# A hybrid decoder layer on one core: TensorE's instructions in the order in which the program writes them

## The chip, the core and the metric

The kernel runs on one core of a Trainium2 chip. What counts is the device time of one execution in microseconds (us); the time before is the median of three runs. The engines have short names in the rows: PE is TensorE (matmul), PEld its weight loads, DVE is VectorE, ACT is ScalarE, POOL is GpSimd, SP is SyncE, whose queue issues most loads.

## What is computed

One layer of a hybrid decoder (width 1024) over a prompt of 2048 positions and over 8 single samples that share the weights:

```python
h = rmsnorm(x, norm1_g)
z = h @ w_in                               # 2432 columns, split among four mixers
ya = chunk_gmlp(zau, zav, ...)             # 128-position chunks, causal W_s per head
yb = s5_ssm(zbu, ...)                      # 16 groups x 64 complex states
yc = short_conv(zcx, zcb, zcc, ...)
yd = rwkv7(zd, ...)                        # 4 heads x 64, delta rule
x = x + concat(ya, yb, yc, yd) @ w_out
x = x + (silu(gate) * up) @ w_down         # gate, up = rmsnorm(x) @ w_gu
y = rmsnorm(x)
```

Inside rwkv7 the key `kk` is normalised by head, a state matrix is carried from position to position, and a bonus is added to its normalised output:

```python
kk = kk / jnp.maximum(jnp.linalg.norm(kk, axis=-1, keepdims=True), 1e-12)
bonus = jnp.sum(rf * kf * r_k, axis=-1, keepdims=True) * vf
out = (on + bonus) * g
```

## The kernel before

**Large products.** The prompt is cut into four pieces of 512 positions. Every weight matrix is used in split precision: a 128x128 weight tile is cast (`wh`, ACT, L176) and its remainder is taken (`wl`, DVE, L177), and one k-tile costs three matmuls of 512 columns, one of the high parts (L214) and two of bf16 parts (L218), all written by `mmg`. The 8 samples ride in the columns of one piece (the last in the output projection and the FFN, there in two blocks of 260; piece 1 in the z projection). These products I call large. Weights stream in through SP's queue into three raw buffers. PSUM is cut into 4 buffers for large products (`m`), 3 for the mixers (`x`) and 1 for small sums (`ms`).

**The stages.** A prelude norms the input, projects the z columns of all pieces (those of pieces 1 and 2 are parked in DRAM), sets up the S5 matrices (`s5_setup`) and runs the mixers of piece 0. Then stage q runs the output projection, the second norm and the FFN of piece q (22 tiles `up`/`down`), and beside it the mixers of piece q+1. The last stage has no mixers. In the windows below the stretches are the prelude (0 to 557 us, up to the first lora product of the next piece), stages 0, 1 and 2 (to 1041, 1614 and 2218 us) and the last stage.

**A mixer.** RWKV works on half pieces z0 and z1 of 256 positions. `rw_a` makes the decay, the gates and the normalised key: lora products (L920), squares of the key (ACT), their sum by head (L960), square root, reciprocal, then the bonus product (L977) and scans. `rw_b` transposes, builds the matrix `BD` (L1069, L1070), multiplies it (L1074, L1075) and inverts a 32x32 triangle on POOL (L1103, L1105). `rw_c` is the recurrence, 8 chunks one after the other, each a chain of TensorE and DVE steps: L1128 (state times `RB`), DVE L1131, L1132 (times the inverse `Y`), copies L1133/L1134, then L1137 and L1146. `rw_d` norms the output and turns it back (L1173). `zrest` holds the gMLP (L796 among its products) and the convolution, `s5` the four groups of the state space.

**What sets the order.** A tile scheduler orders the instructions of all five engines: it simulates them with its own costs and picks by priority (`tc.high_priority(offset=...)`). The table `todo` only says at which FFN tile a mixer's part is written into the program; where its matmuls end up among the large ones the scheduler decides. Each engine then runs its own list in order, and waits on semaphores for the other engines.

Of the kernel before, what the change touches and what calls it, by code (L numbers as in the profile page):

```python
# [17 lines left out]
P = 128  # L18
# [47 lines left out]
def trunk(ctx: ExitStack, tc: tile.TileContext, I, O):  # L66
# [21 lines left out]

    def nm(s):
        uid[0] += 1  # L90
        return f"{s}_{uid[0]}"
# [46 lines left out]
    with tc.high_priority(offset=60000):  # L138
        pv = const.tile([P, NPV], F32, name="c_pv")
        nc.scalar.dma_start(pv, I["pv"])  # L140
# [12 lines left out]
    with tc.high_priority(offset=60000):  # L153
# [14 lines left out]
    def weights(srcs, hp=None):  # L168
        parts = [[] for _ in srcs]
        for i, (src, pl) in [(i, x) for i in range(2) for x in zip(srcs, parts)]:  # L170
            with tc.high_priority(offset=hp[i] if hp else HP):
# [32 lines left out]
    def mmg(jobs, mixed=False):  # L204
# [6 lines left out]
        for run in runs:  # L211
            for i, ps, blk, (wh, _, _), (xh, _, _) in run:
                for p_, (c0, n) in zip(ps, blk):
                    T.matmul(p_[:, :n], lhsT=wh, rhs=xh[:, c0 : c0 + n], start=i == 0, stop=False)  # L214
            for i, ps, blk, (_, wb, wl), (_, xb, xl) in run:
                for a, b, e in ((wl, xb, False), (wb, xl, True)):
                    for p_, (c0, n) in zip(ps, blk):
                        T.matmul(p_[:, :n], lhsT=a, rhs=b[:, c0 : c0 + n], start=False, stop=e and i == ends[id(ps)])  # L218

# [33 lines left out]
    def rms(rs, w, E_=G, pst=mst):  # L253
# [3 lines left out]
        nb = len(starts)  # L257
        ps = pst()
# [9 lines left out]
        newton(r, mc, EPS, st16()[:, :nb], E_)  # L268
        for c0 in [P * b for b in range(nw)] + ([P * nw] if nw < nb else []):
            n = min(P, w - c0)  # L270
            if c0 == TP:
                S.copy(rs[:, :TP], ps)
            o = ps[:, c0 % TP : c0 % TP + n]
            b = c0 // P
            T.matmul(o, lhsT=rt[:, b : b + 1].to_broadcast([P, P]), rhs=ident[:, P - n :], start=True, stop=True)
        c0 = TP if w > TP else 0
        S.copy(rs[:, c0:w], ps[:, : w - c0])
        return rs, rt, ps
# [18 lines left out]
    def norm0():  # L297
# [3 lines left out]
        for i in range(2):  # L301
            with tc.high_priority(offset=(30000, 5000)[i]):
# [7 lines left out]
        with tc.high_priority(offset=-2000):  # L310
            return h, rms(squares(lambda k: xs[k], TP, at_, True), TP)
# [17 lines left out]
    with tc.high_priority(offset=20000):  # L329
        h, (rs0, rt0, _) = norm0()  # L330
# [12 lines left out]

    wsum = mst()
    for i in range(4):
        T.matmul(wsum[64 * (i % 2) : 64 * (i % 2) + 64, P * (i // 2) : P * (i // 2) + P],
                 lhsT=ones.to_broadcast([P, 64]), rhs=wst[:, i], start=True, stop=True)
    for j in range(2):
        t = tri[:, P * j : P * j + P]
        V.tensor_scalar(t, wsum[:, P * j : P * j + P], 1024.0, col("gl", j), op0=ALU.mult, op1=ALU.mult)  # L350
        V.tensor_tensor(bsb[:, j], bsb[:, j], t, op=ALU.add)
# [48 lines left out]


# [7 lines left out]
    def s5_setup():  # L409
        with ExitStack() as c2:  # L410
# [120 lines left out]
            def cmul(ore, oim, ar, ai, br_, bi_):  # L531

                tt(tmp, b16(ar), br_, ALU.mult)
                tt(tmp2, b16(ai), bi_, ALU.mult)
                tt(ore, tmp, tmp2, ALU.subtract)
                tt(tmp, b16(ar), bi_, ALU.mult)
                tt(tmp2, b16(ai), br_, ALU.mult)
                tt(oim, tmp, tmp2, ALU.add)
# [44 lines left out]
            for i in range(2):  # L583
# [8 lines left out]
                Fz.append(f_)  # L592
            for pr in range(8):
# [4 lines left out]
                for g in range(2):  # L598
                    ps_ = slice(64 * g, 64 * g + 64)
                    for ri in range(2):  # L600
# [4 lines left out]
                        else:  # L605
                            act(cv[ps_, ri, g], bc[ps_, 3, pr], AF.Copy, scale=-1.0)
                            act(fv[ps_, ri, :, g], Ft[ps_, 1, pr], AF.Copy, scale=-1.0)
                pe = mst()
# [39 lines left out]

    def park(h, q):
# [22 lines left out]
    def zload(h, m, q, off=0):  # L672
# [4 lines left out]
        for p_, (c0, n) in zip(ztile(h, m, q), zblocks(q)):  # L677
            if q == 0 and m < 2:
                S.copy(t[:, off + c0 : off + c0 + n], p_[:, :n])
                V.tensor_tensor(t[:, off + c0 : off + c0 + n], t[:, off + c0 : off + c0 + n], rs0[:, c0 : c0 + n], op=ALU.mult)  # L680
            elif q == 0:
# [5 lines left out]
    def zrw(h, q):  # L687
        w = zwidth(q)
        zs = rw.tile([P, 7, TP], F32, tag="zs", name=nm("zs"))

# [23 lines left out]
    def zrest(h, q, cct):  # L714
# [14 lines left out]

# [5 lines left out]
        pst = mst if q in parked else mmt  # L735
        uu = [] if q in parked else [gate(j) for j in range(2)]
        if q not in parked:
            wv = [weight(I["wv"][i]) for i in range(2)]
        vn = []
        for g, (b0, nb, rows) in enumerate(groups(q)):  # L740
            vt = zt_() if rows == P else vs
            n = 256 * nb
            if q in parked:
                nc.sync.dma_start(vt[:rows, :n], zdr[q - 1, 17 + g, :rows, :n])
                act(vt[:rows, :n], vt[:rows, :n], AF.Gelu_apprx_tanh)
            else:
                ps = zav(h, b0 * P, nb, rows, wv)
                for b in range(nb):
                    act(vt[:, b * 256 : b * 256 + 256], ps[:, b * 256 : b * 256 + 256],
                        AF.Gelu_apprx_tanh, scale=rt0[:, b0 + b : b0 + b + 1])  # L750
            for b in range(nb):
                vb = vt[:rows, b * 256 : b * 256 + 256]
                bn = st16()
                V.bn_stats(bn[:rows, 0:6], vb)
                V.bn_aggr(bn[:rows, 6:8], bn[:rows, 0:6])
# [867 lines left out]
```

## Time and profile before

| | before |
|---|---|
| median of 3 runs | 2649.69 us (2646.79 to 2650.6) |
| the profiled execution | 2644.79 us, its span 2643.0 us |
| PE busy | 2451.2 us, 93% of the span |
| DVE busy | 1781.7 us, 67% |
| ACT busy | 1063.5 us, 40% |
| POOL busy | 935.9 us, 35% |
| mean granted clock of TensorE | 0.955 of full |

The span runs from the first to the last instruction. An engine that is busy for 93% of it is the one that sets the time; what is left to win on it are its waits, the time in which it ran at the lower clock, and the work itself.

### The profile page before, as it was taken

The page shows a single profiled execution, that of the slowest core. Times are in us where ns is not written, and L with a number is a line of the kernel's source. Part 1 is how long each engine was busy: PE and PEld are TensorE (multiplying, and loading weights), DVE is VectorE, ACT ScalarE, POOL GpSimd, SP SyncE. Part 2 cuts the span into 40 slices and gives each one's busy share as a digit, 9 for nine tenths or more (in the row PEclk, how much of TensorE's full clock was granted, in tenths as well). Part 3 has the DMA queues.
Part 4 walks back from the last instruction along what each step waited for, and adds up shares of the span by engine and source line. Part 5 has one row for each costly group of instructions (what it writes and reads, how often), then busy time and mean ns, then how long its engine had stood idle before and what let it go on. Part 6 is the DMA issues. An engine that isn't in the chain of part 4 may idle for free.

```text
span 2643.0 us, 39426 instructions
## 1 busy us (share of the span) xinstructions
PE 2451.2 (93%) x13863; PEld 1632.7 (62%) x14020; DVE 1781.7 (67%) x3213; ACT 1063.5 (40%) x2173; POOL 935.9 (35%) x1358
## 2 busy tenths in 40 slices
PE   7778989999889999999899999989899999999998
PEld 4557975655455654555555545655455557888887
DVE  6694463488677667876776668556876686566666
ACT  5543443453433334444333345533443335322223
POOL 8588350035346112471371133351362114111102
PEclk9798999999879999999899998999999999999999
DMA  4224444432313223423232235332432234232332
GB/s 135 77 80 153 163 131 133 145 100 76 117 51 109 86 89 116 141 74 121 70 114 81 91 120 160 108 115 85 124 110 84 92 94 158 91 97 93 96 93 80
DMA packets 179606, 280.94 MB, mean 106 GB/s; under 512 B 39208, under 2 KB 53584, under 8 KB 179408
## 3 DMA queue, kind: packets, MB, share of 16 engines
q1 hardware_dynamic: 161648, 254.50, 31.0%
q10 hardware_dynamic: 17760, 23.91, 2.6%
q8 instruction: 110, 1.80, 0.3%
q14 instruction: 88, 0.72, 0.1%
HBM read 250.24 MB, written 28.10 MB: 105 GB/s over the span
## 4 chain that ended last, share of the span: by engine, by line
PE 60%; POOL 14%; DVE 11%; issue 5%; DMA 4%; ACT 3%; SPq 0%; ACTq 0%; POOLq 0%; DVEq 0%
PE m L218 34%; PE m L214 18%; POOL BD L1105 4%; POOL inv L1103 4%; DVE wl L177 2%; POOL s5Q L423 1%; DVE g L867 1%; PE x L1137 1%; PE x L1146 1%; DMA z<-zdr 1%; PE x L1074 1%; POOL inv L423 1%; PE x L1128 1%; DVE xm L1290 1%; DMA x<-in_xq 1%
## 5 line engine op out<-in xcount | busy, mean ns | idle before, releaser
L218 PE MATMUL m<-rl,wh 128*128 128x512 bf16 (+1 forms) x2741 | 839.7, 337 | 9.6 <-DVE rl L284 1.7
L177 DVE TENSOR_TENSOR wl<-raw,wh 128x512 bf16<-128x512 f32 x744 | 571.4, 777 | 394.3 <-ACT wh L176 390.3
L218 PE MATMUL m<-rh,wl 128*128 128x512 bf16 (+1 forms) x2660 | 832.1, 345 | 2.2 <-issue 0.9
L176 ACT CAST wh<-raw 128x512 fp32r<-128x512 f32 x744 | 450.4, 617 | 937.9 <-PE m L218 699.0
L214 PE MATMUL m<-rh,wh 128*128 128x512 f32 (+1 forms) x2760 | 643.8, 374 | 30.5 <-ACT rh L197 15.1
L218 PEld LDWEIGHTS <-wl 128*128 128x128 bf16 x3640 | 351.3, 98 | 368.5 <-issue 119.5
L214 PEld LDWEIGHTS m<-rh,wh 128*128 128x128 f32 x2760 | 452.4, 192 | 126.3 <-ACT rh L197 18.9
L218 PEld LDWEIGHTS <-wh 128*128 128x128 bf16 x3640 | 361.1, 99 | 232.0 <-issue 15.2
L1273 POOL TENSOR_TENSOR gr<-gp,rs 128x512 f32<-128x512 f32 (+1 forms) x110 | 144.5, 1321 | 722.9 <-DVE gp L1271 641.9
L214 PE MATMUL m<-ah,wh 128*128 128x512 f32 (+1 forms) x880 | 289.9, 419 | 22.7 <-DVE xm L1290 11.2
L1290 DVE TENSOR_TENSOR xm<-m,xm 128x512 f32<-128x512 f32 (+1 forms) x440 | 249.0, 581 | 91.5 <-PE m L218 89.9
L218 PE MATMUL m<-al,wh 128*128 128x512 bf16 (+1 forms) x877 | 287.3, 342 | 3.2 <-issue 0.7
L218 PE MATMUL m<-ah,wl 128*128 128x512 bf16 (+1 forms) x845 | 285.2, 352 | 0.6 <-DVE wl L177 0.5
L1127 POOL TENSOR_SCALAR stl<-st,g 128x64 f32<-128x64 f32 x128 | 73.2, 587 | 348.3 <-DVE st L1140 344.5
L214 PEld LDWEIGHTS m<-ah,wh 128*128 128x128 f32 x880 | 151.1, 193 | 67.5 <-DVE xm L1290 18.1
L1103 POOL TENSOR_TENSOR inv<-BD 32x30 f32<-32x30 f32 (+14 forms) x240 | 148.1, 617 | 74.4 <-DMA BD<-dl 56.2
L1105 POOL TENSOR_TENSOR BD<-BD,inv 32x30 f32<-32x30 f32 (+14 forms) x240 | 155.0, 646 | 18.3
L244 POOL TENSOR_TENSOR rs<-rs,at 128x512 f32<-128x512 f32 (+1 forms) x53 | 76.7, 1448 | 114.4 <-ACT at L133 110.7
L1274 DVE SCALAR_TENSOR_TENSOR ft<-ft,gr 128x512 f32<-128x512 f32 (+1 forms) x110 | 77.2, 716 | 52.3 <-POOL gr L1273 47.1
L1271 DVE TENSOR_TENSOR gp<-m,rs 128x512 f32<-128x512 f32 (+1 forms) x110 | 62.3, 582 | 23.5 <-PE m L218 21.2
L1276 ACT CAST ah<-ft 128x512 fp32r<-128x512 f32 (+1 forms) x88 | 54.7, 621 | 52.5 <-DVE ft L1275 50.1
L1275 DVE SCALAR_TENSOR_TENSOR ft<-ft,m 128x512 f32<-128x512 f32 (+1 forms) x110 | 61.9, 578 | 20.5 <-PE m L218 20.1
(371 smaller groups left out, 2800.8 us busy)
## 6 DMA issues: line engine op xcount, KB each, us to landing
raw<-in_wgu SPq DMA_DIRECT2D x352, 256.0 KB, 2.6
raw<-in_wd SPq DMA_DIRECT2D x176, 256.0 KB, 2.6
raw<-in_wz SPq DMA_DIRECT2D x136, 256.0 KB, 2.7
raw<-in_wo SPq DMA_DIRECT2D x64, 256.0 KB, 2.7
x<-in_xq SPq DMA_DIRECT2D x40, 256.0 KB, 3.1
zdr<-zp ACTq DMA_DIRECT2D x33, 256.0 KB, 2.2
z<-zdr SPq DMA_DIRECT2D x33, 256.0 KB, 3.3
xm<-in_xq SPq DMA_DIRECT2D x24, 256.0 KB, 4.0
```

The lines of the kernel that those rows point to most:

```text
L176: S.copy(hi, raw)
L177: (G if spare[0] and i > 9 else V).tensor_tensor(lo, raw, hi.bitcast(F32), op=ALU.subtract)
L214: T.matmul(p_[:, :n], lhsT=wh, rhs=xh[:, c0 : c0 + n], start=i == 0, stop=False)
L218: T.matmul(p_[:, :n], lhsT=a, rhs=b[:, c0 : c0 + n], start=False, stop=e and i == ends[id(ps)])
L244: G.tensor_tensor(acc[:, :w], acc[:, :w], sq[:, :w], op=ALU.add)
L1103: G.tensor_tensor(tv, xtv[:, 0:s, s : s + 1].to_broadcast([32, s, r]), xtv[:, s : s + 1, s + 1 :].to_broadcast([32, s, r]), op=ALU.mult)
L1105: G.tensor_tensor(xtv[:, 0:s, s + 1 :], xtv[:, 0:s, s + 1 :], tv, op=ALU.add)
L1127: G.tensor_scalar(stl[:, j], old[:, j], pvw[:, 8 * j + c, 32:33], None, op0=ALU.mult)
L1271: V.tensor_tensor(gp[:, c], pss[0][b][:, :n], rs[:, c], op=ALU.mult)
L1273: G.tensor_tensor(gr[:, c], gp[:, c], rs[:, c], op=ALU.mult)
L1274: V.scalar_tensor_tensor(tv, tv, 1.0, gr[:, c], op0=ALU.add, op1=ALU.mult)
L1290: V.tensor_tensor(xm[m][:, c0 : c0 + n], p_[:, :n], xm[m][:, c0 : c0 + n], op=ALU.add)
```

## The change

TensorE is taken out of the scheduler: within `tc.manual_schedule` its instructions run in the order in which the program writes them. The other four engines are still ordered by the scheduler.

The order is now made in the program. A mixer's part, a norm or a gate is a Python generator in a `Strand`, and it yields a number where it needs the result of another engine. `mmg` calls `tick` after each large product (a product of 512 columns counts 1, of 256 one half), and `tick` resumes every strand whose number has run out. So between two steps of a strand stand a fixed count of large products, if there are any: `Strand.done` and `finish` run what is left of a strand with none between. RWKV yields 50 between the squares of the key and L1097 (L960 before), 36 and then 24 and 10 in `rw_b`, 13 at each of the three steps of a chunk (10 in piece 0), 36 before the transposes of `rw_d`; a norm yields 24 between its sums (L326) and its broadcast (L342).

Besides that:
- The bonus product (L977) moves from `rw_a` to `rw_tail`, the end of the half piece (L1134); the two lora products of a half are issued together.
- At the start, the first four z tiles of piece 0 are written ahead of the first norm's remaining steps (`ahead0`). The first two z columns of piece 0 are no longer copied by ACT before they are scaled.
- 48 products of 128x128 elements in `s5_setup` (`cmul`) go from POOL to DVE, as does one multiply of piece 0's keys per half; some adds of the second norm's squares and its last steps go to DVE as well. In all DVE runs 82 more TENSOR_TENSOR, 8 more TENSOR_SCALAR and 8 fewer SCALAR_TENSOR_TENSOR, POOL 74 and 8 fewer; ACT loads its table 66 times instead of 57. TensorE's matmuls and the DMAs stay the same in number.
- The gate bias, the final multiplies of the pieces and the samples' mixer become strands too.

Core of the diff:

```diff
+    ctx.enter_context(tc.manual_schedule(engines={mybir.EngineType.PE}))
...
+    def tick(n=1.0):
+        now[0] += n
+        for t in list(strands):
+            if not t.over and t.wake <= now[0]:
+                t.step()
...
             for i, ps, blk, (wh, _, _), (xh, _, _) in run:
                 for p_, (c0, n) in zip(ps, blk):
                     T.matmul(p_[:, :n], lhsT=wh, rhs=xh[:, c0 : c0 + n], start=i == 0, stop=False)
+                tick(sum(n for _, n in blk) / 512)
...
-                tt(tmp, b16(ar), br_, ALU.mult)
+                V.tensor_tensor(tmp, b16(ar), br_, op=ALU.mult)
...
+        if q == 0:
+            ahead0.extend(ztile(h, m, q) for m in range(4))
+            first.done()
...
+        yield 50 if n == 256 else 20
+        yield from free()
         ps = pst()
         T.matmul(ps[:, : 2 * n], lhsT=blk1, rhs=sq, start=True, stop=True)
...
-    def bonus(zs, c0, n, kf, out, t, pst):
+    def bonus(zs, c0, n, kf, t):
...
-        ps = pst()
-        T.matmul(ps[:, : 2 * n], lhsT=blk1, rhs=t, start=True, stop=True)
...
+        ps = pst()
+        T.matmul(ps[:, : 2 * n], lhsT=blk1, rhs=bon, start=True, stop=True)
...
+        gap = 10 if q == 0 else 13
         for c in range(8):
...
+            yield gap
             T.matmul(pu[:, :64], lhsT=Y[:, c], rhs=z_, start=True, stop=True)
...
+    m.done()
     spare[0] = False
...
-            todo = {0: [nx.a1], 2: [nx.c0], 4: [nx.b1], 5: [nx.rest], 8: [lambda: nx.s5(0)], 9: [lambda: nx.s5(1)],
-                    10: [lambda: nx.s5(2)], 11: [lambda: nx.s5(3)], 13: [nx.c1]}
...
+            if nx and i == 3:
+                nx.start_rest()
...
+            nx.done()
```

In RWKV's strand (`rwkv` in class `Mix`) the parts now follow as:

```python
z0 = yield from rw_a(q, 0, self.zs)
yield from rw_b(z0)
yield 24
z1 = yield from rw_a(q, 1, self.zs)
yield 180
yield from rw_c(z0)
...
yield from rw_b(z1)
...
yield 250
yield from rw_c(z1)
```

**TensorE, the end of the recurrence.** Before, in stage 0, the last chunks of piece 1's second half stand in TensorE's list without a large product between them (`st` is the state, `Y` the inverse):

```order
L1128 MATMUL x_6326<-st_6300,RB 128x64 x2
L1132 MATMUL x_6327<-z_6325,Y 128x64
L1137 MATMUL x_6328<-uv_5302,bt_5317 128x64
L1146 MATMUL x_6326<-uv_5302,sc_5316 128x64
L1137 MATMUL x_6328<-uv_5302,bt_5317 128x64
L1146 MATMUL x_6326<-uv_5302,sc_5316 128x64
L1128 MATMUL x_6349<-st_6323,RB 128x64 x2
```

The changed kernel has the same recurrence as lines L1275, L1280, L1286 and L1295; this is one chunk of the same half in stage 0, with the FFN's products (`m`) around it:

```order
L1275 MATMUL x_6815<-st_6718,RB 128x64 x2
L269 MATMUL m_6836<-rh_5780,wh_6826 128x512 x4
L269 MATMUL m_6836<-rh_5780,wh_6832 128x512 x4
...
L274 MATMUL m_6836<-rl_5781,wh_6826 128x512
L1280 MATMUL x_6816<-z_6814,Y 128x64
L274 LDWEIGHTS wl_6827
...
L269 MATMUL m_6888<-rh_5780,wh_6878 128x512 x3
L1286 MATMUL x_6817<-uv_5457,bt_5472 128x64 x2
L1295 MATMUL x_6815<-uv_5457,sc_5471 128x64 x2
L269 MATMUL m_6888<-rh_5780,wh_6878 128x512
L269 MATMUL m_6888<-rh_5780,wh_6884 128x512 x4
```

From L1275 to L1280 stand 14 large products now, from L1280 to L1286 13, and from L1295 to the next L1275 13.

**DVE, the start of the program.** Before, the first z tile that is taken out of PSUM on DVE (L682, `m` times the norm's `rs`) stands ahead of the samples' state products that need `s5s`, a result of `s5_setup` on POOL:

```order
L697 SCALAR_TENSOR_TENSOR zs_257<-z_288,c_pv,z_258 128x512
L696 TENSOR_TENSOR z_336<-z_294 128x512
L682 TENSOR_TENSOR z_339<-m_352,rs_154 128x512
L177 TENSOR_TENSOR wl_481<-raw_478,wh_480 128x512
L697 SCALAR_TENSOR_TENSOR zs_257<-z_336,c_pv,z_294 128x512
L696 TENSOR_TENSOR z_380<-z_339 128x512
L848 TENSOR_TENSOR ns_7647<-s5s,c_s_226 128x16
L851 TENSOR_TENSOR ns_7647<-s5s,c_s_226 128x16
L848 TENSOR_TENSOR ns_7803<-s5s,c_s_226 128x16
```

In the changed kernel all twelve state products (L971 to L976) stand ahead of the first such z tile, now L778:

```order
L232 TENSOR_TENSOR wl_466<-raw_463,wh_465 128x512
L971 TENSOR_TENSOR ns_7877<-s5s,c_s_198 128x16
L974 TENSOR_TENSOR ns_7877<-s5s,c_s_198 128x16
...
L975 TENSOR_TENSOR ns_8117<-s5s,c_s_198 128x16
L976 TENSOR_TENSOR ns_7877<-ns_7877 128x16
L976 TENSOR_TENSOR ns_8117<-ns_8117 128x16
L778 TENSOR_TENSOR z_387<-m_230,rs_156 128x512
L795 TENSOR_TENSOR z_391<-z_387 128x512
L778 TENSOR_TENSOR z_397<-m_267,rs_156 128x512
```

The twelve moved from behind the first z tile to ahead of all of them. On TensorE 96 large products (four tiles of 24, one for each `m` buffer) can be written before a buffer has to come free.

**TensorE, the end of the prelude.** In the changed kernel `m.done()` writes what is left of piece 0's second half behind the last large product of the prelude:

```order
L274 MATMUL m_4987<-wl_4902,rh_3763 128x256
L1280 MATMUL x_5040<-z_5038,Y 128x64
L1286 MATMUL x_5041<-uv_3648,bt_3663 128x64 x2
L1295 MATMUL x_5039<-uv_3648,sc_3662 128x64 x2
L1275 MATMUL x_5073<-st_5036,RB 128x64 x2
...
L1275 MATMUL x_5096<-st_5070,RB 128x64 x2
L1280 MATMUL x_5097<-z_5095,Y 128x64
L1286 MATMUL x_5098<-uv_3648,bt_3663 128x64 x2
L1295 MATMUL x_5096<-uv_3648,sc_3662 128x64 x2
L1324 MATMUL x_5127<-c_ident,g_5116 128x128 x4
L1134 MATMUL x_5140<-g_1386,c_blk_101 128x512
L1043 MATMUL x_5147<-zs_229,c_lora 128x256 x2
```

What stands there without a large product between is two thirds of a chunk, two whole chunks, `rw_d`'s turn (L1324), the bonus (L1134) and the last lora product (L1043); before, those chunks stood among the z projection's products.

## Rows read from the trace of the kernel before

**Rows 1.** The page: busy us (share of span) and instructions by engine.

```profile
PE 2451.2 (93%) x13863; PEld 1632.7 (62%) x14020; DVE 1781.7 (67%) x3213; ACT 1063.5 (40%) x2173; POOL 935.9 (35%) x1358
```

**Rows 2.** Windows of the five stretches: busy us, granted clock, DMA share.

```profile
core 0: us, PE busy (x) PEld busy (x) DVE busy (x) ACT busy (x) POOL busy (x), PEclk, DMA share, GB/s
0.00:557.00 557.00, 487.72 (x2872) 344.62 (x2894) 325.94 (x615) 248.73 (x563) 285.27 (x523) 0.92 0.41 127
557.00:1041.00 484.00, 449.47 (x2164) 271.57 (x2205) 346.33 (x638) 187.43 (x389) 164.27 (x230) 0.93 0.29 89
1041.00:1614.00 573.00, 523.85 (x2465) 306.93 (x2509) 418.98 (x699) 238.88 (x469) 226.73 (x282) 0.95 0.34 108
1614.00:2218.00 604.00, 578.30 (x2854) 345.11 (x2904) 418.86 (x738) 252.22 (x495) 189.29 (x247) 0.99 0.34 106
2218.00:2643.00 425.00, 411.91 (x3519) 364.42 (x3518) 271.63 (x525) 136.22 (x259) 70.31 (x79) 0.99 0.31 96
```

**Rows 3.** Windows of four stretches with the clock at 0.50, and their sum.

```profile
...
724.70:758.80 34.10, 22.78 (x91) 17.93 (x89) 19.72 (x68) 6.76 (x23) 10.02 (x33) 0.50 0.11 32
sum 92.20, PE 64.28 PEld 49.74 DVE 59.37 ACT 32.26 POOL 32.21; mean PE 16.07 PEld 12.43 DVE 14.84 ACT 8.07 POOL 8.05
```

**Rows 4.** Waits of PE: line, releaser, us in total, times, longest.

```profile
PE x L977 <- DVE g L974: 22.7, 4, 10.1
...
PE ms L796 <- DVE z L759: 14.1, 3, 7.1
...
PE x L1173 <- DVE g L1170: 6.3, 1, 6.3
```

**Rows 5.** PE timeline: start, us, work, in brackets idle before and releaser.

```profile
725.53 0.69 PE L1132 MATMUL x<-z,Y 128*128 128x64 f32 x2 [0.54 <-DVE z L1131]
...
730.16 0.69 PE L1132 MATMUL x<-z,Y 128*128 128x64 f32 x2 [0.54 <-DVE z L1131]
```

**Rows 6.** PE timeline, one z tile of 24 products.

```profile
74.66 2.21 PE L214 MATMUL m<-rh,wh 128*128 128x512 f32 x8
76.72 0.40 PE L218 MATMUL m<-rh,wl 128*128 128x512 bf16 x1
```

**Rows 7.** Window of 21 bf16 products of 512 columns.

```profile
76.70:81.36 4.66, 4.59 (x21) 2.04 (x22) 1.61 (x2) 0.00 (x0) 4.19 (x10) 1.00 0.21 68
```

**Rows 8.** PE and ACT timeline: lora products, then the squares for L960.

```profile
1040.60 1.14 PE L920 MATMUL x<-zs,c_lora 32*128 32x256 f32 x8
...
1066.04 0.50 ACT L133 ACTIVATE g<-zs,c_pv 128x256 f32<-128x256 f32 x1
...
556.90 1.14 PE L920 MATMUL x<-zs,c_lora 32*128 32x256 f32 x8
...
570.60 0.91 ACT L133 ACTIVATE g<-zs,c_pv 128x256 f32<-128x256 f32 x2
```

**Rows 9.** PE and DVE timeline: L960, then the half's last BD write.

```profile
1079.37 1.02 PE L960 MATMUL x<-g,c_blk 128*128 128x512 f32 x2
...
1109.39 0.84 DVE L1069 TENSOR_TENSOR BD<-g,g 64x256 f32<-64x256 f32 x2
...
1630.57 1.02 PE L960 MATMUL x<-g,c_blk 128*128 128x512 f32 x2
...
1648.86 0.42 DVE L1069 TENSOR_TENSOR BD<-g,g 64x256 f32<-64x256 f32 x1
```

**Rows 10.** PE, POOL and DVE timeline of the start.

```profile
5.28 0.80 PE L214 MATMUL m<-rh,wh 128*128 128x512 f32 x1 [5.28 <-ACT rh L133]
...
17.16 0.69 POOL L418 TENSOR_SCALAR t<-s5raw 128x8 f32<-128x8 f32 x1 [3.79 <-DMA s5raw<-in_s5l]
...
45.02 0.36 POOL L423 TENSOR_TENSOR s5s<-t,t 128x8 f32<-128x8 f32 x2
...
45.26 0.18 DVE L848 TENSOR_TENSOR ns<-s5s,c_s 128x16 f32<-128x16 f32 x1 [1.76 <-POOL s5s L423]
```

**Rows 11.** Groups of POOL by line: count, busy us, mean ns, idle before.

```profile
L423 POOL TENSOR_TENSOR s5tmp<-s5s,s5G 128x128 f32<-128x128 f32 x12 | 7.2, 622 | 0.5
```

More of the change, by code (lines that the diff above doesn't have):

```diff
@@ L87, in trunk, with __init__, __enter__, __exit__ @@
     uid = [0]
+    ctx.enter_context(tc.manual_schedule(engines={mybir.EngineType.PE}))
+    offs = [0]
+    strands = []
+    now = [0.0]
+    class hp:
+        def __init__(self, o):
+            self.o = o
+        def __enter__(self):
+            self.cm = tc.high_priority(offset=self.o - offs[0])
+            self.old, offs[0] = offs[0], self.o
+            self.cm.__enter__()
+        def __exit__(self, *a):
+            self.cm.__exit__(*a)
+            offs[0] = self.old
+    class Strand:
+        def __init__(self, gen, prio, wait=0.0, norm=False):
+            self.gen, self.prio, self.wake, self.over = gen, prio, now[0] + wait, False
+            self.norm = norm
+            strands.append(self)
+        def step(self):
+            with hp(self.prio):
+                d = next(self.gen, None)
+            if d is None:
+                self.over = True
+                strands.remove(self)
+            else:
+                self.wake = now[0] + d
+    def tick(n=1.0):
[3 more added lines that the diff above has]
+                t.step()
+    def finish(*ts):
+        while any(not t.over for t in ts):
+            for t in [t for t in strands if t in ts or t.norm]:
+                if not t.over:
+                    t.step()
+    def wait_for(*cond):
+        while not all(c() for c in cond):
+            yield 4
     def nm(s):
@@ L218, in mmg @@
                         T.matmul(p_[:, :n], lhsT=a, rhs=b[:, c0 : c0 + n], start=False, stop=e and i == ends[id(ps)])
+                tick(sum(n for _, n in blk) / 256)
     def newton(r, m, eps, t, E_=G):
@@ L399, in trunk, with gate_bias @@
     parked = set()
+    def gate_bias():
+        yield from ms_free()
+        wsum = mst()
+        for i in range(4):
+            T.matmul(wsum[64 * (i % 2) : 64 * (i % 2) + 64, P * (i // 2) : P * (i // 2) + P],
+                     lhsT=ones.to_broadcast([P, 64]), rhs=wst[:, i], start=True, stop=True)
+        for j in range(2):
+            t = tri[:, P * j : P * j + P]
+            V.tensor_scalar(t, wsum[:, P * j : P * j + P], 1024.0, col("gl", j), op0=ALU.mult, op1=ALU.mult)
+            V.tensor_tensor(bsb[:, j], bsb[:, j], t, op=ALU.add)
     s5_e = dr.tile([8, P, 256], F32, name="s5_e")
@@ L963, in rw_elem @@
         V.reciprocal(sq, sq)
[L964 removed]
+        (G if n == 256 and not first else V).tensor_tensor(kkn, kkn, sq, op=ALU.mult)
         kf = sq
@@ new lines, in start, with start_rest, take, rwkv @@
+        def start(self, wait=0):
+            self.rw = Strand(self.rwkv(), RP, wait)
+        def start_rest(self, wait=0):
+            self.ot = Strand(self.others(), MP, wait)
+        def take(self):
+            if self.cct is None:
+                self.cct = ring_tile()
+            return self.cct
+        def rwkv(self):
+            q = self.q
+            yield from wait_for(lambda: all(f.over for f in finals))
+            z0 = yield from rw_a(q, 0, self.zs)
[4 more added lines that the diff above has]
+            yield from rw_c(z0)
+            yield from wait_for(lambda: self.cct is not None)
+            yield from rw_d(z0, self.cct)
+            yield from rw_b(z1)
+            self.half = True
+            yield 250
+            yield from rw_c(z1)
+            yield from wait_for(lambda: self.s5_over)
+            yield from rw_d(z1, self.cct)
@@ L1451, in trunk @@
-    for pg in range(4):
-        m.s5(pg)
-    if last > 1:
-        with tc.high_priority(offset=2 * RP):
-            h1 = norm1(2, rs1)
-        with tc.high_priority(offset=-LOW):
-            park(h1, 2)
-    m.c1()
+    with hp(MP):
+        n1 = Rms(norm1_squares(1), zwidth(1), prio=MP, wait=100)
+    with hp(MP):
+        m.gm2 = m.rest()
+        next(m.gm2)
+    with hp(2 * RP):
+        h = norm1(1, n1.done())
+    m.start_rest(30)
+    if last > 1:
+        with hp(MP):
+            n1 = Rms(norm1_squares(2), zwidth(2), prio=MP, wait=200)
```

455 lines of the change are left out of this document (254 added, 201 removed).

## The prediction

> **What bounds the kernel.** I read the busy shares first, then windows cut at the stage borders, then TensorE's waits, then single places in the timeline. TensorE is busy 2451.2 us of 2643.0, DVE 1781.7 [rows 1]: TensorE sets the time. The windows [rows 2] show where it does not work at full rate: it idles 69.3 us in the prelude (557.00 less 487.72), then 34.5, 49.2, 25.7 and 13.1 us. The granted clock adds a second loss. It stands at one of two levels, so a mean of 0.92 over 557 us means 2 x 0.08 x 557 = 89 us at half clock; for the other windows 68, 57, 12 and 9 us. In four long half-clock stretches TensorE is busy 64.28 of 92.20 us [rows 3], 70%; half of that work time would be saved at full clock, so a half-clock us costs about 0.35 us: 31, 24, 20, 4 and 3 us. (Bounds: if all idle time lies in half-clock time, the prelude loses 10 us this way; if none, 45. The others 17 to 34, 4 to 29, 0 to 6.) Idle and clock loss together are 100, 58, 69, 30 and 16 us, 273 in all; the rest, about 2370 us, is work that the change does not touch, since TensorE's matmuls stay the same in number.
>
> The waits have no single cause. The largest is the bonus product, 22.7 us in four waits, the longest 10.1; others are the gMLP product (14.1 in three) and the end of a half piece (6.3) [rows 4]. Where the recurrence runs out of large products it takes 4.63 us a chunk (730.16 less 725.53) [rows 5]; the stretch in which it does so, 724.7 to 758.8, has the clock at 0.50 and 22.78 of 34.10 us busy [rows 3].
>
> **The change, part by part.** The measure of cover is the large product. A z tile's 8 products of the high parts take 76.72 less 74.66, 0.26 us each [rows 6], 21 bf16 products 4.66 us, 0.22 each [rows 7]; over a tile of 24 that is 0.233 us, the price of one tick.
>
> *Recurrence.* Three hops of 13 ticks give a chunk 9.1 us of large products, against 4.63 us that it needs alone. In stages 0 to 2 every chunk stands so, and their waits and most half-clock time in these stretches should go.
>
> *Key norm.* 50 ticks are 11.7 us. From the lora products to the squares it takes 24.8 us in one half (1041.74 to 1066.54) and 13.5 in another (558.04 to 571.51) [rows 8]. The first is at a loose place, where nobody hurried DVE; I take a shortfall of 2 us a half, bounds 0 and 13.2.
>
> *BD.* From L960 to the last write of BD it takes 29.8 us (1080.39 to 1110.23) or 17.7 (1631.59 to 1649.28) [rows 9]; 36 and 24 ticks are 14.0 us. Shortfall 3.7 by the tighter row, 15.8 by the other, 0 if the scheduler puts this chain ahead of its other DVE work; I take 3.
>
> *Bonus.* At the end of its half nothing waits between its operands and itself, so the 22.7 us of [rows 4] go. Its result is now needed at once by the multiply in the tail, which only the output product waits for; in stages that is hidden by the FFN.
>
> *Other strands* (norms, gMLP, S5, the FFN's own evacuations). A single gMLP wait is 4.7 us today [rows 4]. I leave 8 us a stage, bounds 2 and 16.
>
> So stages 0, 1 and 2 keep 2 x 2 + 2 x 3 + 8 = 18 us of waits and 4 of half clock, 22 each. They gain 36, 47 and 8. The last stage has no mixer and gains nothing.
>
> *The prelude* gains less, for two places. At the start TensorE begins at 5.28 us and can write 96 products before it needs a buffer: 22.4 us, and some 3 more at its early rate, so it stands at about 31. The evacuation it needs is now behind the state products that want `s5s`, which POOL writes at 45.02 to 45.38 [rows 10]. That is a wait of 14 us that was not there before (the first z tile was taken ahead of those). Bounds: 8 if the S5 load, waited for 3.79 us at 17.16 [rows 10], comes earlier, 20 if POOL, which now does the norm later, is later too. At the end, 2.7 chunks of 4.63 us, `rw_d` with a wait like the 6.3 us at L1173 [rows 4], and a tail that I put at 5 us stand alone: 24 us, at a clock that falls. The first 5.3 us stay, the two halves of piece 0 fall short by 12 together (their counts are shorter), 7 for the rest, 5 of half clock: 5 + 14 + 24 + 12 + 7 + 5 = 67, a gain of 33.
>
> *Work moved to DVE.* 48 products of 128x128 leave POOL, where such ones took 0.622 us with little idle time before them [rows 11]. On DVE they add at most 48 x 0.62 = 30 us to 1781.7; TensorE waits for neither, as the S5 matrices are wanted late, so I cost them at nothing. If that cover is gone, a few of the 30 us appear in the prelude. The Trainium skill says in "SBUF — State Buffer", section "SBUF: two separate sides", that DVE and GpSimd share a port pair under an exclusive lock: a DVE instruction with two SBUF inputs and a GpSimd instruction wait for each other in full. By it each moved product could be held for one POOL instruction, another 30 us of DVE time and up to that much on the total; no row here separates such holding from work, and the sum goes without it.
>
> Sum: 33 + 36 + 47 + 8 = 124. The profiled execution took 2644.8 us, 1.8 more than its span, and lies 4.9 below the median of the three runs. 2644.8 - 124 = 2521, and 2526 on the median's scale; I say 2525.
>
> **The rivals.**
> (a) *The cover suffices nearly everywhere.* For it: the last window idles only 13.1 us of 425 with a written-like list. Then a stage keeps 5 us instead of 22 and the prelude 39 (start, tail, 10 for the rest): gains 61 + 53 + 64 + 25 = 203, 2447 on the median's scale. Against it: the counts of [rows 8] and [rows 9].
> (b) *The waits move to the queues of DVE and ACT.* These still run their own lists in the order that the scheduler thinks right, and each hop needs one result from them. In stage 1 DVE is busy 418.98 of 573 us [rows 2]. If each of the 3 x 16 x 3 = 144 hops of the stages misses its time by 0.5 us, as now at L1132 (0.54 [rows 5]), that is 72 us: 2598.
> (c) *Slower: a late small product holds all large ones behind it.* Today the scheduler placed a mixer's product late enough for its own model; now TensorE stands in front of it. Place: L1097 and the first product of BD, in each of eight halves. With the loose durations, 13.2 and 15.8 us short, a half loses 29 instead of the 4 to 6 taken above: some 190 us more, 2715. It decides from about 15 us more a half on, half of that difference. Against it: these durations were loose because nothing on TensorE waited for them. The Trainium skill ("TensorE: Matmul & The Clock Gate", section "The mechanism") says that matmuls start and end strictly in order and only weight loads are pulled ahead, which is what would make each such wait count in full; the trace agrees at the bonus product, where nothing ran for 10.1 us.
> (d) *The change does little:* the scheduler's other four lists hold the waits as they are, 2640 to 2655.
>
> **How the numbers follow.** My forecast, with 2475 to 2570 as its own range, has 0.50; (a) 0.22, (b) 0.20, (c) 0.05, (d) 0.03. The range runs from 2440, (a) with a little more, to 2600, the end of (b); it leaves out (c), (d) and the ends of (a) and (b), under 2 in 10. About 0.2% (5 us) is what a measurement of this kernel can tell from no change. Faster: 0.50 + 0.22 + 0.20 and a little of (d), 0.93; same 0.02; slower 0.05.
>
> **What would show it.** Right: no wait at the bonus product; chunks of 9 us with large products in them and a granted clock of 0.98 or more from 557 us on; idle time of stages 0 to 2 under 25 us each; a wait of some 14 us of TensorE for an `m` buffer before 46 us; 24 us of idle and half clock at the prelude's end. Wrong: waits of 10 us and more at L1097 or L1219 in most halves (c), many short ones at L1280 and L1286 (b), or a prelude as long as before.

## The result

The changed kernel takes 2711.47 us (median, 2707.71 to 2714.41), the kernel before 2648.34 in the same session: a ratio of 1.0237, interval [1.0219, 1.0255]. It is slower by some 63 us where I forecast 124 us less. The span of the profiled execution grew from 2643.0 to 2709.7 us, by 66.7.

The page of the kernel after, its engines' busy time, which answers to [rows 1]:

```profile
PE 2453.5 (91%) x14020; PEld 1630.7 (60%) x14020; DVE 1809.0 (67%) x3295; ACT 1083.9 (40%) x2188; POOL 882.4 (33%) x1276
```

TensorE is busy 2453.5 us, as before (2451.2); what grew is the time in which it is not, from 191.8 to 256.2 us. Both kernels have one landmark at the same work: the first result of the output projection of stage 0, and the last result of the down projection of stages 0, 1 and 2. Windows cut there, first of the kernel before, then of the one after (busy us by engine, granted clock, DMA share, GB/s):

```profile
0.00:522.00 522.00, 452.91 (x2719) 325.81 (x2739) 293.16 (x568) 231.12 (x525) 269.77 (x512) 0.91 0.40 127
522.00:1058.80 536.80, 499.14 (x2378) 297.38 (x2420) 396.80 (x710) 217.10 (x459) 190.82 (x250) 0.94 0.30 93
1058.80:1582.20 523.40, 485.67 (x2316) 286.57 (x2357) 379.74 (x649) 210.20 (x410) 202.86 (x261) 0.96 0.33 102
1582.20:2207.20 625.00, 590.82 (x2844) 348.76 (x2897) 432.28 (x757) 259.89 (x509) 194.21 (x254) 0.97 0.34 108
2207.20:2643.00 435.80, 422.71 (x3612) 374.13 (x3611) 279.75 (x534) 145.16 (x274) 78.20 (x85) 0.99 0.32 101
```

```profile
0.00:550.00 550.00, 455.45 (x2746) 324.34 (x2747) 323.54 (x642) 232.59 (x537) 240.90 (x467) 0.89 0.39 123
550.00:1071.90 521.90, 481.18 (x2405) 289.37 (x2404) 381.46 (x685) 217.76 (x442) 182.40 (x236) 0.97 0.31 95
1071.90:1610.00 538.10, 484.73 (x2365) 286.03 (x2363) 381.46 (x664) 226.66 (x430) 195.55 (x253) 0.95 0.32 99
1610.00:2258.10 648.10, 595.08 (x2898) 349.34 (x2899) 442.48 (x767) 262.45 (x511) 192.26 (x247) 0.96 0.33 103
2258.10:2709.70 451.60, 437.05 (x3612) 381.59 (x3610) 280.08 (x542) 144.43 (x271) 71.26 (x75) 0.99 0.30 96
```

The prelude lost 28.0 us (550.0 against 522.0), stage 0 won 14.9, stage 1 lost 14.7, stage 2 23.1 and the last stage 15.8. In the prelude and in stages 1 and 2 the difference is idle time for the most part: 94.6 instead of 69.1, 53.4 instead of 37.7, 53.0 instead of 34.2 us. In stage 0 idle time grew a little too (40.7 instead of 37.7); what it won is busy time, 18.0 us less, at a clock of 0.97 instead of 0.94. Elsewhere the clock did not rise: 0.89 in the prelude, 0.95 and 0.96 in stages 1 and 2, against 0.91, 0.96 and 0.97. In the last stage the loss is not idle time: TensorE idles 14.6 instead of 13.1 us there, and is busy 14.3 us longer for as many matmuls (3612).

What TensorE waits for now, the answer to [rows 4] (line, releaser, us in total, times, longest):

```profile
PE m L269 <- ACT rh L252: 53.1, 24, 5.7
PE x L1097 <- ACT g L188: 35.4, 6, 9.0
PE ms L902 <- DVE z L883: 29.5, 3, 13.2
PE x L1219 <- DVE BD L1213: 20.1, 3, 12.2
PE m L269 <- DVE xm L1453: 18.1, 9, 6.5
...
PE x L1219 <- issue: 6.4, 1, 6.4
...
PE x L1280 <- DVE z L1278: 5.7, 5, 2.5
```

The bonus product is gone from the list, and the recurrence (L1280) is low. In their place stand five kinds: the parts `rh` of the normed input of the next piece, 53.1 us; the key norm's product L1097, 35.4 in six of eight halves; the gMLP product L902, 29.5 in all three stages; the first product of BD, L1219, 26.5 (with the 6.4 for which the trace shows no releaser); and evacuations of the FFN. The parts `rh` were waited for before as well, but less:

```profile
PE m L214 <- ACT rh L197: 15.1, 9, 5.9
```

Of the changed kernel's 53.1 us most are in the prelude; the same row for its window 0 to 550:

```profile
PE m L269 <- ACT rh L252: 39.6, 16, 5.7
```

### The profile page after: what moved, and what is told of

Its sections match the earlier page's. It is cut to its first block, busy times and chain, and to the rows that moved or that the text cites. A ratio compares the mean times of both kernels' runs of the same rounds, so it can differ in the third digit from the quotient of the medians.

```text
span 2709.7 us, 39564 instructions
## 1 busy us (share of the span) xinstructions
PE 2453.5 (91%) x14020; PEld 1630.7 (60%) x14020; DVE 1809.0 (67%) x3295; ACT 1083.9 (40%) x2188; POOL 882.4 (33%) x1276
## 4 chain that ended last, share of the span: by engine, by line
PE 65%; POOL 11%; DVE 11%; DMA 5%; issue 4%; ACT 3%; SPq 0%; POOLq 0%; ACTq 0%; DVEq 0%
PE m L274 37%; PE m L269 20%; POOL BD L1251 4%; POOL inv L1249 4%; DVE wl L232 2%; DMA x<-in_xq 2%; PE x L1219 1%; DMA z<-zdr 1%; DVE g L986 1%; PE x L1295 1%; PE x L1286 1%; PE x L1275 1%; ACT wh L231 1%; POOL rs L301 1%; PE ms L1034 1%
## 5 line engine op out<-in xcount | busy, mean ns | idle before, releaser
L274 PE MATMUL m<-rh,wl 128*128 128x512 bf16 (+1 forms) x2760 | 875.5, 350 | 0.0
L274 PE MATMUL m<-rl,wh 128*128 128x512 bf16 (+1 forms) x2760 | 849.3, 340 | 2.6 <-DVE rl L372 2.6
L269 PE MATMUL m<-rh,wh 128*128 128x512 f32 (+1 forms) x2760 | 651.4, 376 | 68.5 <-ACT rh L252 53.1
L1453 DVE TENSOR_TENSOR xm<-m,xm 128x512 f32<-128x512 f32 (+1 forms) x440 | 246.3, 581 | 105.0 <-PE m L274 95.8
L269 PE MATMUL m<-ah,wh 128*128 128x512 f32 (+1 forms) x880 | 249.7, 399 | 35.9 <-DVE xm L1453 16.0
L274 PE MATMUL m<-al,wh 128*128 128x512 bf16 (+1 forms) x880 | 273.2, 341 | 1.6 <-DVE al L1440 1.6
L1249 POOL TENSOR_TENSOR inv<-BD 32x30 f32<-32x30 f32 (+14 forms) x240 | 154.6, 644 | 197.3 <-DMA BD<-dl 130.6
L301 POOL TENSOR_TENSOR rs<-rs,at 128x512 f32<-128x512 f32 (+1 forms) x41 | 58.3, 1422 | 71.7 <-ACT at L188 70.8
L1438 DVE SCALAR_TENSOR_TENSOR ft<-ft,m 128x512 f32<-128x512 f32 (+1 forms) x110 | 61.9, 579 | 25.2 <-PE m L274 24.4
```

The costliest lines, as they stand in the source:

```text
L301: G.tensor_tensor(acc[:, :w], acc[:, :w], sq[:, :w], op=ALU.add)
L1249: G.tensor_tensor(tv, xtv[:, 0:s, s : s + 1].to_broadcast([32, s, r]), xtv[:, s : s + 1, s + 1 :].to_broadcast([32, s, r]), op=ALU.mult)
L1453: V.tensor_tensor(xm[m][:, c0 : c0 + n], p_[:, :n], xm[m][:, c0 : c0 + n], op=ALU.add)
```

## The experiments

Times are medians, and each ratio is to the kernel before in the same session. That kernel's own median went from 2643.81 to 2648.34 us between sessions, so a difference of two medians can be off by some 4 us; where that matters I give the difference by the ratios as well.

**Give TensorE back to the scheduler.** First with nothing else changed:

```diff
-    ctx.enter_context(tc.manual_schedule(engines={mybir.EngineType.PE}))
```

> The changed kernel with TensorE given back to the scheduler; all other edits stay. If the written order of TensorE is what costs (theory A), the 64 us of extra idle time go with it: 2620 to 2655 us. If the other edits (work moved to DVE, the strands' later writing of norms and final multiplies, the longer lists of DVE and ACT) are what costs (theory B), it stays at 2690 or above.

2685.96 us, 1.0152 [1.0136, 1.0169]: between the two theories, and not a clean undo. Its windows show why: prelude 611.3 us, stage 0 501.2. The change had also raised the priority of the parked z columns, which says nothing to a written list of TensorE, but much to the scheduler: as I read it, it finished them first and left piece 0's mixers alone at the end. So once more, with that priority as before:

```diff
-    ctx.enter_context(tc.manual_schedule(engines={mybir.EngineType.PE}))
...
-    with hp(2 * RP):
+    with hp(-LOW):
         park(h, 1)
...
-        with hp(2 * RP):
+        with hp(-LOW):
             park(h, 2)
```

> As the run with TensorE given back to the scheduler, and the parked z columns of pieces 1 and 2 put back to low priority as in the kernel before. That run lost 89 us in the prelude and won 35 and 12 in stages 0 and 1. If the prelude's loss was that priority alone: 2640 to 2655, as the kernel before. If the changed program is slower whoever orders TensorE: 2675 to 2690.

2601.54 us, 0.984 [0.982, 0.9861]: faster than either kernel, and outside both expectations. Its prelude takes 504.8 us. So the other edits are worth some 42 us under the scheduler, and the written order with these counts costs 110 us against the scheduler in nearly the same program; the lower priority of the parked columns holds for the other four engines too, and no run tried it with the written order. How the scheduler avoids the waits is seen where the key norm is latest. PE and ACT timeline of that version in stage 1: lora products, the squares, the key norm's product (here L1096):

```profile
1015.71 1.31 PE L1042 MATMUL x<-zs,c_lora 32*128 32x256 f32 x8
...
1070.35 0.91 ACT L187 ACTIVATE g<-zs,c_pv 128x256 f32<-128x256 f32 x2 [0.36 <-DVE g L1077]
...
1071.31 1.13 PE L1096 MATMUL x<-g,c_blk 128*128 128x512 f32 x2 [0.97 <-ACT g L187]
```

From the lora products' end to the squares' it took 54.2 us, and TensorE waited 0.97 us: the scheduler had put the product as late as its operands. The same place in the changed kernel:

```profile
1086.02 1.14 PE L1043 MATMUL x<-zs,c_lora 32*128 32x256 f32 x8
...
1106.54 0.91 ACT L188 ACTIVATE g<-zs,c_pv 128x256 f32<-128x256 f32 x2 [0.33 <-DVE g L1078]
...
1107.50 2.07 PE L1097 MATMUL x<-g,c_blk 128*128 128x512 f32 x2 [8.98 <-ACT g L188]
```

Here the squares end 20.3 us after the lora products, much sooner, and TensorE waits 8.98: it stands after 50 large products, 11.7 us, whatever the other engines do.

**The bonus product alone**, moved in the kernel before:

```diff
-        bonus(zs, c0, n, kf, bon, tb, mxt)
+        bonus(zs, c0, n, kf, bon)
...
         ps = pst()
+        T.matmul(ps[:, : 2 * n], lhsT=blk1, rhs=bon, start=True, stop=True)
+        for j in range(2):
+            V.tensor_tensor(bon[:, j * n : j * n + n], ps[:, j * n : j * n + n], zs[:, 5 + j, c0 : c0 + n], op=ALU.mult)
+        ps = pst()
         lora_mm(ps, 64, 128, zs, c0, n)
```

> The kernel before with the bonus product alone moved to the end of its half piece. If the 22.7 us of waits at the bonus product were a loss of their own: 2622 to 2635 us. If the scheduler merely parked other late products there (the next wait takes over): 2643 to 2655.

2646.85 us, 1.0004 [0.9994, 1.0013]: nothing. Its 22.7 us of waits were a place where the list stood anyway; other waits took over, such as that of the recurrence for the inverse (4.8 us in the kernel before), here L1131:

```profile
PE x L1131 <- DMA Y<-dx: 19.0, 4, 9.8
```

In the scheduler's version of 2601.54 us I made the move back (the same edit the other way round):

> The version of 2601 us (scheduler orders TensorE, parked columns last) with the bonus product moved back to its old place. If the move helps in this program: 2610 to 2625. If it is worth nothing, as in the kernel before: 2597 to 2606.

2609.53 us, 0.9859 [0.9844, 0.9874]: between the two expectations, 8 us slower by the medians and 5 by the ratios, whose intervals overlap; so a gain from the move is not clear of noise. The bonus product (here L1113) waits again:

```profile
PE x L1113 <- DVE g L1110: 23.1, 4, 8.1
```

And the small products of the S5 set-up, put back on GpSimd in that version:

```diff
-                V.tensor_tensor(tmp, b16(ar), br_, op=ALU.mult)
+                tt(tmp, b16(ar), br_, ALU.mult)
...
-        (G if n == 256 and not first else V).tensor_tensor(kkn, kkn, sq, op=ALU.mult)
+        (G if n == 256 else V).tensor_tensor(kkn, kkn, sq, op=ALU.mult)
```

> The same version with the 48 small products of the S5 set-up and piece 0's key multiply back on GpSimd. If moving them to DVE is what shortens its prelude by 17 us: 2612 to 2625. If not: 2597 to 2606.

2614.46 us, 0.9878 [0.9863, 0.9892]: 13 us by the medians, 10 by the ratios, the first expectation. I had costed that move at nothing.

**The last stage: one output tile per group.**

```diff
-            g = 2
+            g = 2 // len(bl)
```

> The changed kernel; in the last stage the down projection takes one output tile (two PSUM buffers) per group of products instead of two (all four buffers). If the last stage is longer by 15.8 us because each group needs all four buffers back at once: 2695 us, and 859 instead of 827 matmuls per 100 us in its middle. If it is longer for another reason (weights, DVE): no change, 2711.

2698.97 us, 1.0205 [1.0188, 1.0222]. The median fell by 12.5 us (8.5 by the ratios), the last window from 451.7 to 435.7. One hundred us from the middle of the last stage, of the kernel before, the changed one and this one (matmuls in brackets):

```profile
2400.00:2500.00 100.00, 100.00 (x859) 88.48 (x858) 65.12 (x126) 29.29 (x54) 11.43 (x12) 1.00 0.30 94
```

```profile
2455.00:2555.00 100.00, 100.00 (x829) 87.13 (x827) 61.72 (x119) 28.16 (x52) 11.39 (x12) 1.00 0.29 94
```

```profile
2440.00:2540.00 100.00, 100.00 (x863) 89.30 (x861) 64.39 (x126) 29.11 (x54) 11.40 (x12) 1.00 0.30 95
```

All three are 100% busy at full clock, yet the changed kernel gets 829 matmuls done instead of 859; with one tile per group it is 863. The down projection writes groups of two output tiles by two blocks, so each group begins with eight high products into all four `m` buffers. TensorE and DVE timeline of the changed kernel, the high products of two groups and the emptying of the buffers between them (L1453):

```profile
2484.93 1.61 PE L269 MATMUL m<-ah,wh 128*128 128x260 f32 x8
...
2488.13 1.61 PE L269 MATMUL m<-ah,wh 128*128 128x260 f32 x8
...
2487.39 1.67 DVE L1453 TENSOR_TENSOR xm<-m,xm 128x260 f32<-128x260 f32 x4 [1.53 <-PE m L274]
...
2488.30 0.43 DVE L1453 TENSOR_TENSOR xm<-m,xm 128x260 f32<-128x260 f32 x1
...
2488.78 0.72 PE L269 MATMUL m<-ah,wh 128*128 128x260 f32 x2
```

The last two rows are single records out of the merged ones: the third emptying, and the fifth and sixth high product.

The kernel before, where the scheduler had put two high products at a time:

```profile
2400.08 0.49 PE L214 MATMUL m<-ah,wh 128*128 128x260 f32 x2
...
2400.79 0.49 PE L214 MATMUL m<-ah,wh 128*128 128x260 f32 x2
```

And the run with one tile per group:

```profile
2441.31 0.72 PE L269 MATMUL m<-ah,wh 128*128 128x260 f32 x4
2442.71 0.72 PE L269 MATMUL m<-ah,wh 128*128 128x260 f32 x4
```

A group of 24 products takes 3.20 us in the changed kernel (2488.13 less 2484.93); as many take 2.84 us before (four times 0.71) and 2.80 with one tile per group (twice 1.40). The last stage has 44 such groups, so by these rows an estimated 16 to 18 us, where the windows show 15.8 and 16.0. That it is the size of the group is shown by the run. That the buffers are what it waits for is seen in the single records: the fifth and sixth high product of a group, the first into its third and fourth buffer, start at 2488.78 and 2489.12, each 0.05 us behind the end of that buffer's emptying (2488.73 and 2489.06). The trace records no idle time for it.

**Longer counts, one at a time.**

```diff
-        yield 50 if n == 256 else 20
+        yield 100 if n == 256 else 20
```

> The changed kernel with 100 instead of 50 large products ahead of the key norm's product L1097. If its 35.4 us of waits come from a chain of some 21 us against 11.7 us of cover: those waits under 8 us, 2680 to 2690. If the wait only moves to the next late step (the first product of BD, the gMLP): 2703 to 2715.

2701.87 us, 1.0219 [1.0204, 1.0235]: 10 us by the medians, 5 by the ratios, neither expectation. L1097 no longer waits at all, but L902 waits 21.6 us more, in the waits of this run:

```profile
PE ms L902 <- DVE z L883: 51.1, 3, 22.8
```

```diff
-        yield 40
+        yield 120
         for j in range(2):
             yield from ms_free()
```

> The changed kernel with 120 instead of 40 large products ahead of the gMLP product L902. If its 29.5 us of waits are a count that is too short: 2685 to 2697. If they pass to the next late step of the same strand: 2703 to 2715.

2692.81 us, 1.0179 [1.0163, 1.0196]: 19 us (15 by the ratios). L902 waits no more, L1097 as before (34.9 us).

**And less cover, the dose the other way.**

```diff
-        yield 50 if n == 256 else 20
+        yield 25 if n == 256 else 20
```

> The changed kernel with 25 instead of 50 large products ahead of the key norm's product, so 5.8 us less cover in each of eight halves. If a wait in a list in written order counts in full: waits at L1097 grow by 35 to 46 us and the time with them, 2735 to 2757. If TensorE's waits merely shift between steps: 2705 to 2722.

2735.22 us, 1.0335 [1.0319, 1.035]: 24 us slower, at the edge of the first expectation. Its waits:

```profile
PE x L1097 <- ACT g L188: 80.9, 8, 17.0
...
PE ms L902 <- DVE z L883: 13.6, 3, 6.4
```

L1097 waits 45.5 us more, close to eight times the 5.8 us that were taken away. L902 waits 15.9 less and L1219 13.0 less, as I read it because their chains get on while TensorE stands at L1097; L1324 waits 17.0 more (22.9). The wait counts in full at its place, and part of it is taken off others.

**Both counts, and three mends.** If a wait at one place shortens waits elsewhere, mending it alone uncovers those, and both mends together are worth more than their sum. At the key norm and the gMLP:

```diff
-        yield 50 if n == 256 else 20
+        yield 90 if n == 256 else 20
...
-        yield 40
+        yield 120
```

> The changed kernel with the two longer counts alone (90 ahead of the key norm, 120 ahead of the gMLP product), the last stage as it was. Apart they gave 10 and 18 us. If each, mended alone, passed its waits on to the other: 2647 to 2656, as the three mends less the last stage's 12 to 16. If the three mends' 73 us need the last stage too: 2675 to 2685.

2655.65 us, 1.003 [1.0017, 1.0044]: 56 us, where apart they gave 10 and 19 (by the ratios 55, 5 and 15). L1097 waits 1.0 us in all, L902 is gone from the list. TensorE's idle time, 256.2 us in the changed kernel, is 253.1 with the key norm mended, 248.4 with the gMLP and 217.4 with both; the other 20.6 us of the span's gain are busy time, at a mean clock of 0.959 instead of 0.949. With the last stage's mend (`g = 2 // len(bl)`) as well:

> The changed kernel with three mends together: the down projection one tile at a time in the last stage, 90 products ahead of the key norm, 120 ahead of the gMLP product. Alone they gave 12, 10 and 18 us. If these are separate losses: 2668 to 2675. If a mended wait passes on to the next late step: 2680 to 2695.

2638.36 us, 0.9969 [0.9957, 0.9982]: 73 us less than the changed kernel, and a little faster than the kernel before, with TensorE in written order. It beat both expectations, the plain sum included.

**The prelude's end.**

```diff
-        gap = 10 if q == 0 else 13
+        gap = 7 if q == 0 else 13
...
-            yield 180
+            yield 60 if q == 0 else 180
...
-            yield 250
+            yield 150 if q == 0 else 250
```

> As the run with three mends, and piece 0's recurrence starts sooner (60 and 150 instead of 180 and 250 products ahead of it, 7 instead of 10 at its hops), so that its end stands among the parked z columns. If the 24 us of half clock and 12 us of idle time at the prelude's end come from those last chunks standing alone: 12 to 20 us faster than that run. If the inverse on GpSimd is not ready by then: TensorE waits at L1280 and it is no faster or slower.

2624.86 us, 0.9917 [0.9899, 0.9935]: 13.5 us less; up to the first output projection it takes 527.9 instead of 557.9 us, of which stage 0 gives 7 back. Its last chunk now stands among the parked columns, where the run with three mends has no large product for 42.6 us (497.8 to 540.4) and the changed kernel for 23.7 (510.7 to 534.4). So the longer counts had lengthened this end, and the 13.5 us are the gain over that. On top of it longer counts in `rw_b`:

```diff
-        yield 36
+        yield 60
...
-            yield (24, 10)[g % 2]
+            yield (40, 16)[g % 2]
```

> As the run with piece 0's recurrence sooner, and 60, 40 and 16 instead of 36, 24 and 10 large products in rw_b. Its waits at the first products of BD are 12.3 us in all. If that is a loss of its own: 2608 to 2618. If the waits pass on, or piece 0's end is late again: 2620 to 2640.

2644.46 us, 1.0003 [0.999, 1.0016]: 20 us slower, a little beyond the second expectation. Every product of cover also delays what follows in its strand. BD no longer waits, but in piece 0's second half the inverse on GpSimd starts at 390.2 instead of 346.9 us, and TensorE stands 15.0 us for it at once:

```profile
PE x L1280 <- DMA Y<-dx: 15.0, 1, 15.0
```

**The normed input earlier.** `norm1` for pieces 1 and 3 is made in a strand of its own, ahead of the last products that don't need it, and the first z weights are asked for behind it:

```diff
+        def done(self):
+            finish(self.n.strand, self.strand)
+            early.extend(weight(I["wz"][m]) for m in range(2))
+            return self.h
...
+            if n1 and i == 21:
+                h = norm1(q + 2, n1.done())
```

> The changed kernel with the normed input h of pieces 1 and 3 made while other large products still run (a strand during the z tiles of piece 0; ahead of stage 1's last down projection) instead of right ahead of its first use; that of piece 2 stays. If the 53 us of waits for its parts (L269 for rh) are lost time: those waits about 12 us, 2670 to 2685. If the loads or DVE are late anyway: 2700 to 2715.

2720.51 us, 1.0285 [1.0267, 1.0303]: slower by 9 (13 by the ratios), beyond both expectations. The waits for `rh` left, all but 2.6 us, and these came:

```profile
PE m L269 <- ACT wh L231: 42.9, 6, 13.3
...
PE m L269 <- ACT zp L772: 25.2, 1, 25.2
```

`norm1` loads its x through the three raw buffers of the weights, so early loads of x can hold back the weights (`wh`); that this is the cause is read from the code and these waits, and not tested by itself. All mends at once with this one among them (counts 100, 120 and the longer ones in `rw_b`):

> The edits of e3, e4, e5 and e6 together, and 60, 40 and 16 instead of 36, 24 and 10 products in rw_b. If the written order is sound and only its counts and three places were wrong, the savings add (16 + 26 + 35 + 22 + 15 us): 2600 to 2630. If the other engines' lists are what TensorE waits for, wherever it waits: 2650 to 2680.

2696.65 us, 1.0195 [1.0172, 1.0217], slower than both expectations, with 55.0 us of waits for `wh`. The same mends without the early input and without `rw_b` (and 90 for 100 at the key norm) are the run of 2638. A version with buffers of its own for x was not tried; so what the 53.1 us of `rh` waits are worth stays open.

## Why the prediction was wrong

The step that failed is how the sum treats idle time. It books all idle time and half-clock cost of the first four stretches as gained and puts back only what I could name: 18 us of waits a stage, 8 of them for "other strands", and 67 us in the prelude. In the three stages, by the windows above, TensorE idles 147.1 us where the sum allowed 54. The two places that I had worked out hold 40 of these, key norm 26.0 and BD 14.3, where I took 12 and 18; the recurrence has 9.5. All else is 97 us, against 24 for "other strands". In the prelude I left 7 us for the rest, and the waits for `rh` alone are 39.6. I put half clock at 5 us there and 4 a stage; at the granted clocks of 0.89, 0.97, 0.95 and 0.96 the four stretches stand at half clock for some 121, 31, 54 and 52 us, by my price of 0.35 an estimated 42, 11, 19 and 18. And I put the last stage at nothing, which lost 15.8.

The mechanism is that of rival (c): in a list in written order a late product holds all large products behind it. I gave it 0.05 and 2715 us; the time is 2711, but that closeness is chance. Its two places make up 61.9 us of waits (L1097 and L1219) where (c) needed 29 us in each of eight halves, 232, and of the waits of 10 us and more that were its sign one came (12.2, at L1219). The rest came from places that I had not priced.

- *Key norm.* I took a shortfall of 2 us a half, because the 24.8 us of [rows 8] were "at a loose place, where nobody hurried DVE". In the changed kernel the chain takes 18.5, 13.7, 14.0, 13.4, 20.3, 18.9, 11.3 and 19.1 us in the eight halves, against 11.7 of cover: TensorE's list hurries nobody either, since DVE and ACT keep lists that the scheduler made for its own idea of time. It waits 35.4 us instead of 16, within my bounds; but with the gMLP's it is the count whose mending gave 56 us.
- *Other strands: the term that failed most.* 8 us a stage for norms, gMLP, S5 and evacuations; the gMLP alone takes 9.8. Its 40 products are counted from where the program writes the convolution's result, and DVE does the norm of its values only later. And I added these terms as if they were independent; the run of 56 us against 10 and 19 shows that they are not.
- *BD.* 3 us a half, 24 in eight, and 26.5 us measured in four waits: the size came out, but 12.2 of it lies in one half of piece 0. Longer counts were no cure.
- *Terms that were missing.* The normed input of the next piece, 53.1 us, where the kernel before waits 15.1 and the scheduler's version of 2601.54 us 17.8. In written order its first product stands right behind its making; that the scheduler let other products run meanwhile is how I read these numbers. And the last stage, which "has no mixer and gains nothing": it lost 15.8 us, because the written order opens all four buffers at once where the scheduler did not.
- *The start.* No wait of 14 us. `s5s` came at 40.05 us instead of 45.02, and TensorE was held before that, 5.2 us at the norm's broadcast (L342, at 37.05 us), so it had not yet filled its buffers when DVE emptied the first at 41.52.
- *The prelude's end.* Right: the last chunks stand alone there, for 23.7 us without a large product, where I had said 24. Moving them under the parked columns gained 13.5 us in the run with three mends.
- *Recurrence.* Right: with 13 products at each hop L1280 and L1286 wait 14.1 us in all. But the granted clock is 0.97, 0.95 and 0.96 in the stages, not the 0.98 or more that I gave as a sign.
- *Bonus.* I booked 22.7 us of waits as if they were a gain; in the kernel before the move alone is worth nothing.
- *Work moved to DVE.* I costed it at nothing; with the key multiply it gains 10 to 13 us where the scheduler orders TensorE. On DVE such a product takes 0.28 us, less than half of what GpSimd took [rows 11]; 46 of the 48 take 0.22 to 0.35 us, and all together 15.9 us where I had bounded them by 30. Two took 1.39 and 1.37 us, each beside a GpSimd product of two inputs, and each ended some 0.15 us behind it. That agrees with the holding of which the Trainium skill warns ("SBUF — State Buffer", "SBUF: two separate sides"); it cost DVE some 2 us, not 30, and was not tested by itself.

DVE timeline of the changed kernel, two of the products moved from GpSimd:

```profile
56.60 0.28 DVE L627 TENSOR_TENSOR s5tmp<-s5s,s5G 128x128 f32<-128x128 f32 x1
56.80 0.28 DVE L628 TENSOR_TENSOR s5tmp<-s5s,s5G 128x128 f32<-128x128 f32 x1
```

DVE and POOL timeline, a long one and what ran beside it (until 70.18 and 70.04 us):

```profile
68.79 1.39 DVE L629 TENSOR_TENSOR s5G<-s5tmp,s5tmp 128x128 f32<-128x128 f32 x1
...
68.72 1.32 POOL L301 TENSOR_TENSOR rs<-rs,z 128x520 f32<-128x520 f32 x1 [1.40 <-ACT z L188]
```

- *Strict order.* The Trainium skill ("TensorE: Matmul & The Clock Gate", "The mechanism") has matmuls start and end in order; the 8.98 us at L1097, with large products behind it, agree. Rival (a) fell with the counts; rival (b) was half right, since TensorE waits for DVE and ACT, but at a few long places, not at 144 short ones.

Two things stay open. With all mends that helped the written order takes 2624.86 us, still 100 more than I forecast, and no run says what the `rh` waits, the largest that are left (50.6 us), are worth. And of the 42 us that the other edits give under the scheduler, the products moved to DVE make 10 to 13 and the bonus's move 8 at most; the rest is not assigned.

## What to carry to other kernels

A written order for one engine takes away the one thing that a scheduler did for free: to put a product where its operands are ready. So take the length of each producing chain from the slowest case in the trace, not from the tightest, and cover that, but not more, since each product of cover delays the rest of its strand (longer counts in `rw_b` cost 20 us). Then mend the short counts together, since a wait at one place hides waits elsewhere, and alone each mend can look worth little. Before an engine is taken from the scheduler, look also at what the scheduler had mixed where nothing seemed to need it, such as groups that claim all accumulators at once.

## What the runs showed of the hardware

A TensorE that is 100% busy at full clock in the trace can still be 4% slower (829 against 863 matmuls of 260 columns in 100 us), with no idle time recorded. Two of 48 DVE products of 128x128 elements took 1.39 and 1.37 us instead of 0.28, each beside a GpSimd product of two inputs.
